# Moving four products of the output norm to VectorE in a decoder layer's last pass

## The chip, the cores and the metric

The kernel runs on one core of a Trainium2 chip. A core has TensorE (matmuls into PSUM), VectorE, ScalarE and GpSimd (elementwise work on SBUF; the first two also read PSUM), and queues that start transfers, of which SyncE's (SP) carries nearly all here. In the profile these are PE (with PEld for the loading of weights), DVE, ACT, POOL and SP. The metric is the device time of one execution in microseconds (us), the median of three runs.

## The reference

A decoder layer on `x` (256 tokens x 2048, float32): an attention part, then a feed-forward part, each as `x + rmsnorm(f(rmsnorm(x)))`. The change is in the end of the feed-forward part, here `y @ w_down` and the norm behind it:

```python
def rmsnorm(x, g):
    xf = x.astype(jnp.float32)
    y = xf * lax.rsqrt(jnp.mean(xf * xf, axis=-1, keepdims=True) + EPS)
    return (y * g.astype(jnp.float32)).astype(x.dtype)
...
    u = causal_dwconv(h @ w_up[l], conv_w[l], conv_b[l])
    gate, val = jnp.split(u, 2, axis=-1)
    y = (jax.nn.gelu(gate, approximate=True) * val) @ w_down[l]
    x = x + rmsnorm(y, post_ffn_g[l])
```

`w_down` is 5632 x 2048. The norm's gain `post_ffn_g` is a row of 2048 numbers, its mean one number per token.

## The kernel before

Float32 matmuls are made of three fp32r products: each operand is split into a high part (a cast on ScalarE) and a low part (source minus high part, on VectorE). For a weight tile these are `whi` and `wlo`; the helper `split` (L312, L313) makes both. A weight tile arrives in `raw` (5 buffers), `extra` (2) or the third part of `tb`, each 128 x 1024 and loaded by the SP queue.

The 5632 hidden columns are made in two halves. Behind each half come two passes over w_down, one for the output columns 0 to 1023 (`n == 0`) and one for 1024 to 2047 (`n == 2`); the sums of the first half wait in `y_sb` (two tiles `t` of 128 tokens, each of 2048 columns), to which those of the second half are added. Columns are counted in chunks of 512, so (t, n) is a token tile and chunk 0 to 3. `fast_pass` makes one pass: it goes through 11 units `u` of two weight tiles. Units 0, 2, 4 and 6 use a Strassen-like scheme with fewer products, whose combined sums (`m1`, `m5`, `m6`, `m7`, banks `bank_acc`) are spread over the outputs by `add_early` (L1121 to L1130); all others add products straight into four banks `late` (`bank_att`), one per (t, chunk).

In the very last pass the last three units (8, 9, 10) are held (`HOLD`): their split weights stay in SBUF, the last unit's in `rest`, and `block(0)` to `block(3)` multiply them at the end, one output block after the other: (0, 2), (0, 3), (1, 2), (1, 3). So the outputs come one by one, and the norm's work for one lies beside the matmuls of the next. Block (1, 3) is made in two halves of 256 columns.

What is done behind the blocks is written out from L1177 on. The order there is the program's on ScalarE, VectorE, GpSimd and SP (`manual_schedule`); before that line a scheduler places the instructions of these engines, except those under `keep_in_program_order`. TensorE's order is the program's throughout. The steps:

- `down(t, n, b, h)`: VectorE adds a bank to `y_sb` (L1087), ScalarE squares the result and sums the squares into `ysq[t]` (L1088).
- `gain(t, n, h, into)`: GpSimd multiplies a chunk of `y_sb` with the gain row `gbf` (L1154). All eight chunks are done so, (1, 3) in two parts, the second one into the tile `last`.
- `before_last(t, n)`: VectorE sums the first n partial sums of squares (L1160) and scales the sum (L1162); `rstd_y` adds the last one (L1167), and GpSimd raises the mean to the power -0.5 (L1169).
- `finish(t, cs, r, q, y)`: VectorE computes `y * r + x_back` (L1173, two tensor inputs in SBUF), and a queue stores it to the output. Tile 0 is finished in four steps of 512 columns, tile 1 in 512, 512, 512, 256, 256.
- `x_back` (the residual) and `gbf` are loaded by SP behind the last weights (L1182, L1184).

Of the kernel before, what the change touches and what calls it, by code (L numbers as in the profile page):

```python
# [8 lines left out]
F32 = mybir.dt.float32  # L9
# [3 lines left out]
ALU = mybir.AluOpType  # L13
# [4 lines left out]
P = 128  # L18
S = 256
D = 2048  # L20
# [11 lines left out]
def hybrid_layer(ctx: ExitStack, tc: tile.TileContext, x, pre_mix_g, w_in, b_forget, sinks,  # L32
# [3 lines left out]
    pe, act, dve, pool, sp = nc.tensor, nc.scalar, nc.vector, nc.gpsimd, nc.sync  # L36
# [7 lines left out]
    small = ctx.enter_context(tc.tile_pool(name="small", bufs=4))  # L44
# [4 lines left out]
    def bank(tag="acc"):  # L49
        return ps.tile([P, 512], F32, tag=tag, bufs=4, name="bank_" + tag)  # L50
# [13 lines left out]
    UNIT = 1024  # L64
# [66 lines left out]
    mhalf = const.tile([P, 1], F32, tag="mhalf", name="mhalf")  # L131
# [13 lines left out]
    for i in range(2):  # L145
        cs = slice(i * 256, (i + 1) * 256)
# [16 lines left out]
    junk = const.tile([P, 512], BF16, tag="junk", bufs=1, name="junk")  # L163
# [151 lines left out]
    with tc.tile_pool(name="mixp", bufs=1) as mp:  # L315
# [315 lines left out]
        for p0, npair, cols in ((0, 3, 384), (3, 3, 384), (6, 2, 272)):  # L631
# [13 lines left out]
            for t, b in enumerate(b2):  # L645
# [79 lines left out]
        gbc = hp.tile([P, D], F32, tag="gbc", name="gbc_mix")  # L725
# [121 lines left out]
    with tc.tile_pool(name="ffn", bufs=1) as fp:  # L847
# [24 lines left out]
        ROOM = 4128  # L872
# [95 lines left out]
                          stop=(last and i == 2))  # L968

        def fast_pass(G, sums, order, k00, c0, load, tb, early, late, add_early, hold=1,  # L970
                      keep=None):

            left, right = slice(0, 512), slice(512, UNIT)
            fast = [u for u in order if u in FAST]
# [19 lines left out]
            for u in order:  # L994
                k = 2 * u
                ra, rb = (load(w_rows(w_down, k00 + k + a, 1, c0, UNIT)) for a in range(2))
                if u in FAST:
# [26 lines left out]
                    if end and hold == 1:  # L1024
                        add_early()
                    continue
                b = [parts(r, UNIT, keep[a] if keep and u == order[-1] else None)
                     for a, r in enumerate((ra, rb))]
                if u in order[-hold:]:
                    held += [(k + a, b[a]) for a in range(2)]  # L1030
                    continue
# [17 lines left out]
        for half in range(2):  # L1049
# [4 lines left out]
            for g in range(FHALF // 2):  # L1054
# [10 lines left out]
                gates, ys = [], []  # L1065
# [18 lines left out]
            def down(t, n, b, h=None):  # L1084
                i, cs = (n, slice(0, 512)) if h is None else (n + h, slice(h * 256, h * 256 + 256))
                ys = y_sb[:, t, n * 512:(n + 1) * 512][:, cs]
                dve.tensor_tensor(ys, b[:, cs], ys, op=ALU.add)  # L1087
                act.activation(junk[:, cs], ys, AF.Square, accum_out=ysq[t][:, i:i + 1])  # L1088

            extra = fp.tile([P, 2, UNIT], F32, tag="gbc", name="extra")  # L1090
            tb = fp.tile([P, 3, UNIT], F32, tag="room", name="tb")
            spare = [extra[:, 0, :], extra[:, 1, :], tb[:, 2, :]]
            loads = [0]

# [8 lines left out]
            for n in (0, 2):  # L1103
# [28 lines left out]
                final = half and n  # L1132
                rest = None
                if final:
                    rest = main.tile([P, 2, 2, UNIT], F32R, tag="hT", name="rest")
                block = fast_pass(G, sums, order, half * FHALF, n * 512, load, tb, early, late,
                                  add_early, HOLD if final else 1,
                                  rest and [[rest[:, a, i, :] for i in range(2)]
                                            for a in range(2)])
# [11 lines left out]
        def gain(t, n, h=None, into=None):  # L1151
            cs = slice(0, 512) if h is None else slice(h * 256, h * 256 + 256)
            ys = y_sb[:, t, n * 512:(n + 1) * 512][:, cs]
            pool.tensor_tensor(ys if into is None else into, ys,  # L1154
                               gbf[:, n * 512:(n + 1) * 512][:, cs], op=ALU.mult)

        def before_last(t, n):

            st = small.tile([P, 1], F32, tag="st", name="st_y")
            dve.tensor_reduce(st, ysq[t][:, 0:n], axis=AX.X, op=ALU.add)  # L1160
            v = small.tile([P, 1], F32, tag="rv", name="rv")
            dve.tensor_scalar(v, st, 1.0 / D, EPS, op0=ALU.mult, op1=ALU.add)  # L1162
            return v

        def rstd_y(t, n, v):
            v2 = small.tile([P, 1], F32, tag="rv", name="rv")
            dve.scalar_tensor_tensor(v2, ysq[t][:, n:n + 1], 1.0 / D, v, op0=ALU.mult, op1=ALU.add)  # L1167
            r = small.tile([P, 1], F32, tag="ry", bufs=2, name="ry")
            pool.tensor_tensor(r, v2, mhalf, op=ALU.pow)  # L1169
            return r  # L1170

        def finish(t, cs, r, q, y=None):
# [7 lines left out]
        x_back = main.tile([P, 2, D], F32, tag="x", name="x_back")  # L1180
        for t in range(2):
            sp.dma_start(x_back[:, t, :], x_dram[t * P:(t + 1) * P, :])  # L1182
        gbf = fp.tile([P, D], F32, tag="gbc", name="gbc_ffn")
        sp.dma_start(gbf, post_ffn_g[0].partition_broadcast(P))  # L1184
        gain(0, 0)
        gain(0, 1)
        block(0)
        down(0, 2, late[0])
        gain(0, 2)
        gain(1, 0)  # L1190
        v = before_last(0, 3)
        block(1)
        down(0, 3, late[1])
        r = rstd_y(0, 3, v)
        gain(0, 3)
        gain(1, 1)
        for n in range(2):
            finish(0, slice(n * 512, (n + 1) * 512), r, sp)
        block(2)
# [2 lines left out]
        for n in range(2, 4):  # L1202
            finish(0, slice(n * 512, (n + 1) * 512), r, sp)
        last = fp.tile([P, 256], F32, tag="last", name="last")
        for h in range(2):
            if h:
                v = before_last(1, 4)
            b = bank()
            block(3, b, slice(512 + h * 256, 768 + h * 256))
            down(1, 3, b, h)  # L1210
            if h == 0:
                gain(1, 3, 0)
        r = rstd_y(1, 4, v)
# [33 lines left out]
```

## Time and profile before

| | |
|---|---|
| median of three runs | 1063.57 us (1063.05 to 1065.51) |
| span of the profiled execution, from first to last instruction (no other time of it is given) | 1062.6 us |
| TensorE busy in the span | 1049.6 us (99%) |
| VectorE | 839.7 us (79%) |
| ScalarE | 639.1 us (60%) |
| GpSimd | 229.3 us (22%) |
| mean granted TensorE clock | 0.996 |

A row of a timeline gives start, duration, engine, line, operation, output and inputs with their shapes, count, and in brackets the idle time of the engine ahead of it with what ended it. A row of several merged operations (x2, x4) gives their time together. [...] Shares of busy time are averages over the span, and here the last 12 us of it matter.

### The profile page before, as it was taken

How to read it: one execution, taken by the hardware profiler on the slowest of the kernel's cores; microseconds unless marked ns; L12 is line 12 of the kernel's file. 1: busy time of each engine (PE TensorE's matmuls, PEld its weight loads, DVE VectorE, ACT ScalarE, POOL GpSimd, SP SyncE). 2: the span in 40 equal slices, each digit the busy share in tenths (PEclk: the TensorE clock that was granted, in tenths of full speed). 3: DMA queues.
4: the chain of work that ended last, by engine and by line, in shares of the span. 5: the costliest groups of instructions: out<-in, count | busy, mean ns of one | idle time of the engine just before them, and what ended most of it. 6: DMA issues, size and time to landing. Idle time of an engine off the chain costs nothing.

```text
span 1062.6 us, 16272 instructions
## 1 busy us (share of the span) xinstructions
PE 1049.6 (99%) x5890; PEld 914.6 (86%) x5890; DVE 839.7 (79%) x1369; ACT 639.1 (60%) x1096; POOL 229.3 (22%) x256
## 2 busy tenths in 40 slices
PE   9999999999999999999999999999999999999996
PEld 7889988888889888888888888888888888888885
DVE  5988887887467887787767999668778687789987
ACT  6767667776556765566655556446556565556551
POOL 4253335441022121211212000002121121200004
PEclk9999999999999999999999999999999999999998
DMA  8745566555773876656665666666566665656563
GB/s 280 217 120 168 162 209 202 165 170 162 282 236 107 280 231 187 193 180 185 211 188 188 193 204 206 213 196 190 169 209 188 197 197 180 194 179 200 194 242 121
DMA packets 154285, 207.08 MB, mean 195 GB/s; under 512 B 6845, under 2 KB 131037, under 8 KB 153181
## 3 DMA queue, kind: packets, MB, share of 16 engines
q1 hardware_dynamic: 153200, 203.37, 60.7%
q10 hardware_dynamic: 1004, 2.68, 0.6%
q8 instruction: 46, 0.75, 0.3%
q14 instruction: 35, 0.28, 0.1%
HBM read 201.68 MB, written 4.21 MB: 194 GB/s over the span
## 4 chain that ended last, share of the span: by engine, by line
PE 84%; DVE 9%; issue 2%; DMA 2%; ACT 2%; POOL 1%; DVEq 0%; SPq 0%; POOLq 0%; ACTq 0%
PE bank_acc L284 15%; PE bank_att L284 14%; PE bank_acc L309 12%; PE bank_att L967 9%; PE bank_acc L290 8%; PE bank_att L290 7%; PE bank_acc L253 7%; DVE wlo L313 4%; PE bank_acc L258 4%; PE bank_acc L967 2%; PE bank_att L475 1%; PE bank_att L510 1%; DVE wlo L115 1%; PE bank_acc L932 1%; DMA raw<-in_w_down_dram 1%
## 5 line engine op out<-in xcount | busy, mean ns | idle before, releaser
L115 DVE TENSOR_TENSOR wlo<-raw,whi 128x1024 fp32r<-128x1024 f32 (+3 forms) x271 | 328.5, 1224 | 127.0 <-ACT whi L112 118.4
L112 ACT CAST whi<-raw 128x1024 fp32r<-128x1024 f32 (+3 forms) x270 | 273.2, 1029 | 131.8 <-issue 88.8
L899 POOL TENSOR_TENSOR room<-room,rowf 128x256 f32<-128x256 f32 x88 | 100.3, 1160 | 393.9 <-DVE room L898 392.0
L284 PE MATMUL bank_acc<-hT,whi 128*128 128x512 f32 x736 | 173.3, 390 | 0.0
L284 PEld LDWEIGHTS bank_acc<-hT,whi 128*128 128x128 f32 x736 | 136.4, 188 | 27.4
L967 PE MATMUL bank_att<-whi,G 128*128 128x512 f32 x488 | 156.0, 389 | 0.0
L284 PE MATMUL bank_att<-hT,whi 128*128 128x512 f32 x640 | 150.6, 390 | 0.0
L284 PEld LDWEIGHTS bank_att<-hT,whi 128*128 128x128 f32 x640 | 118.7, 188 | 23.9
L967 PEld LDWEIGHTS bank_att<-whi,G 128*128 128x128 f32 x488 | 91.6, 188 | 18.9
L967 PE MATMUL bank_att<-wlo,G 128*128 128x512 f32 x244 | 95.0, 389 | 0.2 <-DVE wlo L313 0.2
L290 PEld LDWEIGHTS bank_acc<-hT,wlo 128*128 128x128 f32 x736 | 89.3, 188 | 2.0
L290 PE MATMUL bank_acc<-hT,wlo 128*128 128x256 f32 x736 | 89.8, 279 | 0.0
L901 ACT ACTIVATE room<-room,cw 128x256 f32<-128x256 f32 x88 | 53.0, 602 | 60.6 <-POOL room L899 60.6
L253 PE MATMUL bank_acc<-hT,whi 128*128 128x512 f32 x352 | 88.0, 395 | 0.0
L309 PE MATMUL bank_acc<-whi,oT 128*128 128x512 f32 (+1 forms) x272 | 81.7, 379 | 0.0
L290 PEld LDWEIGHTS bank_att<-hT,wlo 128*128 128x128 f32 x640 | 77.6, 188 | 1.7
L290 PE MATMUL bank_att<-hT,wlo 128*128 128x256 f32 x640 | 77.9, 279 | 0.0
L903 DVE SCALAR_TENSOR_TENSOR room<-room,cw 128x256 f32<-128x256 f32 x88 | 62.4, 709 | 17.6 <-ACT room L901 17.3
L253 PEld LDWEIGHTS bank_acc<-hT,whi 128*128 128x128 f32 x352 | 63.3, 188 | 11.5
L313 DVE TENSOR_TENSOR wlo<-raw,whi 128x1024 fp32r<-128x1024 f32 (+1 forms) x56 | 61.3, 1119 | 12.1 <-ACT whi L312 12.1
L312 ACT CAST whi<-tb 128x1024 fp32r<-128x1024 f32 x42 | 44.0, 1050 | 43.0 <-PE bank_att L967 19.6
L312 ACT CAST whi<-raw 128x1024 fp32r<-128x1024 f32 (+1 forms) x56 | 52.3, 958 | 27.1 <-PE bank_att L967 20.6
(254 smaller groups left out, 1594.0 us busy)
## 6 DMA issues: line engine op xcount, KB each, us to landing
raw<-in_w_up_dram SPq DMA_DIRECT2D x176, 512.0 KB, 4.2
raw<-in_w_down_dram SPq DMA_DIRECT2D x58, 512.0 KB, 4.7
raw<-in_w_in_dram SPq DMA_DIRECT2D x51, 512.0 KB, 4.7
raw<-in_w_out_dram SPq DMA_DIRECT2D x32, 512.0 KB, 4.6
extra<-in_w_down_dram SPq DMA_DIRECT2D x20, 512.0 KB, 4.7
raw<-in_w_in_dram SPq DMA_DIRECT2D x16, 384.0 KB, 3.6
tb<-in_w_down_dram SPq DMA_DIRECT2D x10, 512.0 KB, 3.5
cb<-c_dram SPq DMA_DIRECT2D x8, 256.0 KB, 3.8
```

The source lines that it names most:

```text
L112: i1 = act.copy(hi[:, cs], raw[:, cs])
L115: i2 = dve.tensor_tensor(lo[:, cs], raw[:, cs], hi[:, cs].bitcast(F32), op=ALU.subtract)
L253: pe.matmul(b, parts[u][0][:, a, m * P:(m + 1) * P], hT[:, kt, :], start=(kt == 0), stop=(kt == KT - 1))
L284: pe.matmul(b, parts[u][0][:, a, m * P:(m + 1) * P], hT[:, kt, :], start=(kt == 0), stop=(kt == KT - 1))
L290: pe.matmul(b[:, 256:512], parts[u][1][:, a, m * P:(m + 1) * P], hT[:, kt, 0:256], start=False, stop=False)
L309: pe.matmul(b, a, r[:, cols], start=(first and i == 0), stop=(last and i == 2))
L312: act.copy(hi, src)
L313: dve.tensor_tensor(lo, src, hi.bitcast(F32), op=ALU.subtract)
L899: pool.tensor_tensor(u[:, 2:258], u[:, 2:258], rowf, op=ALU.mult)
L901: act.activation(y, u[:, 2:258], AF.Identity, bias=cw[:, 3, ch:ch + 1], scale=cw[:, 2, ch:ch + 1])
L903: dve.scalar_tensor_tensor(y, u[:, 1:257], cw[:, 1, ch:ch + 1], y, op0=ALU.mult, op1=ALU.add)
L967: pe.matmul(b[:, to] if to else b, a, r[:, cols], start=(first and i == 0), stop=(last and i == 2))
```

## The change

Four things are changed.

1. The products with the gain for chunks 0 and 1 of both token tiles are made by VectorE inside the last pass, one each in units 7, 8, 9 and 10 (`early_gain`, called as `beside` in `fast_pass`). Their values are complete since the pass before. GpSimd keeps (0, 2), (0, 3), (1, 2) and the first half of (1, 3).
2. The gain row is loaded in two halves: columns 0 to 1023 into `gb_lo`, free room behind `tb`, on SP before the last pass; columns 1024 to 2047 where the whole row was loaded before.
3. The mean is no longer taken in two steps for token tile 0: `before_last(0, 4)` sums all four parts after the last square.
4. For the last 256 columns of tile 1 VectorE squares and sums in one operation (`tensor_tensor_reduce`, with the sum of the earlier columns `v` as its start) instead of ScalarE, and VectorE instead of GpSimd makes the product `last`, behind it.

```diff
@@ fast_pass
+                      keep=None, beside=None):
...
                 b = [parts(r, UNIT, keep[a] if keep and u == order[-1] else None)
                      for a, r in enumerate((ra, rb))]
+                if beside:
+                    beside(u)
                 if u in order[-hold:]:
@@ behind each half
             extra = fp.tile([P, 2, UNIT], F32, tag="gbc", name="extra")
-            tb = fp.tile([P, 3, UNIT], F32, tag="room", name="tb")
+            rest_room = fp.tile([P, ROOM], F32, tag="room", name="tb")
+            tb = rest_room[:, 0:3 * UNIT].rearrange("p (a c) -> p a c", a=3)
+            gb_lo = rest_room[:, 3 * UNIT:4 * UNIT]
...
                 final = half and n
                 rest = None
                 if final:
+                    sp.dma_start(gb_lo, post_ffn_g[0, 0:UNIT].partition_broadcast(P))
+
+                def early_gain(u):
+                    if u in (7, 8, 9, 10):
+                        t, c = divmod(u - 7, 2)
+                        ys = y_sb[:, t, c * 512:(c + 1) * 512]
+                        tc.keep_in_program_order(
+                            dve.tensor_tensor(ys, ys, gb_lo[:, c * 512:(c + 1) * 512], op=ALU.mult))
+
+                if final:
                     rest = main.tile([P, 2, 2, UNIT], F32R, tag="hT", name="rest")
...
+                                  final and early_gain)
@@ gain
-                               gbf[:, n * 512:(n + 1) * 512][:, cs], op=ALU.mult)
+                               gbf[:, (n - 2) * 512:(n - 1) * 512][:, cs], op=ALU.mult)
@@ the root
-        def rstd_y(t, n, v):
-            v2 = small.tile([P, 1], F32, tag="rv", name="rv")
-            dve.scalar_tensor_tensor(v2, ysq[t][:, n:n + 1], 1.0 / D, v, op0=ALU.mult, op1=ALU.add)
+        def root(ms):
             r = small.tile([P, 1], F32, tag="ry", bufs=2, name="ry")
-            pool.tensor_tensor(r, v2, mhalf, op=ALU.pow)
+            pool.tensor_tensor(r, ms, mhalf, op=ALU.pow)
             return r
@@ behind the pass
-        gbf = fp.tile([P, D], F32, tag="gbc", name="gbc_ffn")
-        sp.dma_start(gbf, post_ffn_g[0].partition_broadcast(P))
-        gain(0, 0)
-        gain(0, 1)
+        gbf = fp.tile([P, UNIT], F32, tag="gbc", name="gbc_ffn")
+        sp.dma_start(gbf, post_ffn_g[0, UNIT:D].partition_broadcast(P))
         block(0)
         down(0, 2, late[0])
         gain(0, 2)
-        gain(1, 0)
-        v = before_last(0, 3)
         block(1)
         down(0, 3, late[1])
-        r = rstd_y(0, 3, v)
+        r = root(before_last(0, 4))
         gain(0, 3)
-        gain(1, 1)
...
-        for h in range(2):
-            if h:
-                v = before_last(1, 4)
-            b = bank()
-            block(3, b, slice(512 + h * 256, 768 + h * 256))
-            down(1, 3, b, h)
-            if h == 0:
-                gain(1, 3, 0)
-        r = rstd_y(1, 4, v)
-        gain(1, 3, 1, last)
+        b = bank()
+        block(3, b, slice(512, 768))
+        down(1, 3, b, 0)
+        gain(1, 3, 0)
+        v = before_last(1, 4)
+        b = bank()
+        block(3, b, slice(768, UNIT))
+        ys = y_sb[:, 1, D - 256:D]
+        dve.tensor_tensor(ys, b[:, 256:512], ys, op=ALU.add)
+        ms = small.tile([P, 1], F32, tag="ms", bufs=1, name="ms")
+        dve.tensor_tensor_reduce(junk[:, 0:256], ys, ys, 1.0 / D, v, ALU.mult, ALU.add, ms)
+        r = root(ms)
+        dve.tensor_tensor(last, ys, gbf[:, UNIT - 256:UNIT], op=ALU.mult)
```

The lines behind the edits have new numbers: `add_early`'s adds L1123 to L1130 are L1127 to L1134 in the changed kernel, L1087 (the add in `down`) is L1089, the add of the last block's early part L1141 is L1156, L1173 (`finish`) is L1186, and the new products are L1146.

TensorE's, ScalarE's and the queue's orders stay as they were, but for the load of `gb_lo`, one square fewer on ScalarE, and new line numbers. On VectorE the order changes in two places. The first is the end of the last pass. Before (each row: line, operation, output and inputs with the buffer's number, shape):

```order
L313 TENSOR_TENSOR wlo_10470<-extra_9717,whi_10469 128x1024
L313 TENSOR_TENSOR wlo_10500<-extra_9717,whi_10499 128x1024
L313 TENSOR_TENSOR rest_10178<-raw_10521,rest_10178 128x1024
L313 TENSOR_TENSOR wlo_10504<-tb_9718,whi_10503 128x1024
L313 TENSOR_TENSOR wlo_10512<-raw_10507,whi_10511 128x1024
L1123 TENSOR_TENSOR y_sb_3944<-s_10527,y_sb_3944 128x512
L313 TENSOR_TENSOR wlo_10516<-raw_10509,whi_10515 128x1024
L1124 TENSOR_TENSOR s_10527<-bank_acc_10173,s_10527 128x512
```

The first row is the low part of unit 7's second weight tile, the next `wlo` rows and the `rest` row belong to the held units. The same place after:

```order
L313 TENSOR_TENSOR wlo_10471<-extra_9717,whi_10470 128x1024
L1146 TENSOR_TENSOR y_sb_3944<-y_sb_3944,tb_9718 128x512
L313 TENSOR_TENSOR wlo_10502<-extra_9717,whi_10501 128x1024
L313 TENSOR_TENSOR rest_10179<-raw_10525,rest_10179 128x1024
L313 TENSOR_TENSOR wlo_10506<-tb_9718,whi_10505 128x1024
L1146 TENSOR_TENSOR y_sb_3944<-y_sb_3944,tb_9718 128x512
L313 TENSOR_TENSOR wlo_10515<-raw_10510,whi_10514 128x1024
L313 TENSOR_TENSOR wlo_10519<-raw_10512,whi_10518 128x1024
L1146 TENSOR_TENSOR y_sb_3944<-y_sb_3944,tb_9718 128x512 x2
L1127 TENSOR_TENSOR y_sb_3944<-s_10532,y_sb_3944 128x512
```

Two products stand ahead of the last `wlo`, two behind it, and the first add of `add_early` has moved behind all of them. A few rows on, the add of the first held sums (`bank_att_10174`) stands ahead of the last three steps of `add_early`, where before it stood behind them. The second place is the end of the program, VectorE before:

```order
L1160 TENSOR_REDUCE st_y_10651<-ysq1_3946 128x1
L1162 TENSOR_SCALAR rv_10653<-st_y_10651 128x1
L1087 TENSOR_TENSOR y_sb_3944<-bank_acc_10655,y_sb_3944 128x256
L1167 SCALAR_TENSOR_TENSOR rv_10676<-ysq1_3946,rv_10653 128x1
L1173 SCALAR_TENSOR_TENSOR y_sb_3944<-y_sb_3944,ry_10678,x_back_10540 128x512 x3
```

and after, where ISA stands for the one operation that squares and sums, and for the read of its sum:

```order
L1175 TENSOR_REDUCE st_y_10650<-ysq1_3946 128x1
L1177 TENSOR_SCALAR rv_10652<-st_y_10650 128x1
L1221 TENSOR_TENSOR y_sb_3944<-bank_acc_10654,y_sb_3944 128x256
L1223 ISA junk_98,ms_10674<-y_sb_3944,rv_10652 128x256
L1223 ISA ms_10674 128x1
L1225 TENSOR_TENSOR last_10627<-y_sb_3944,gbc_ffn_10548 128x256
L1186 SCALAR_TENSOR_TENSOR y_sb_3944<-y_sb_3944,ry_10676,x_back_10545 128x512 x3
```

The wait for ScalarE's square (ahead of L1167) is gone, two VectorE instructions take its place, and the product `last` has moved here from the end of GpSimd's row.

More of the change, by code (lines that the diff above doesn't have):

```diff
@@ L970, in fast_pass @@
         def fast_pass(G, sums, order, k00, c0, load, tb, early, late, add_early, hold=1,
-                      keep=None):
+                      keep=None, beside=None):
             left, right = slice(0, 512), slice(512, UNIT)
@@ L1138, in hybrid_layer @@
                                   rest and [[rest[:, a, i, :] for i in range(2)]
-                                            for a in range(2)])
+                                            for a in range(2)],
+                                  final and early_gain)
                 if final:
```

## The prediction

> **What bounds the kernel now.** I read the page first, then the busy time by stage, then the end of the chain of waits, and last the timelines of the engines from 1020 us on, since the order of instructions shows that nothing before the last pass over w_down is moved except one load.
>
> ```profile
> span 1062.6 us, 16272 instructions
> PE 1049.6 (99%) x5890; PEld 914.6 (86%) x5890; DVE 839.7 (79%) x1369; ACT 639.1 (60%) x1096; POOL 229.3 (22%) x256
> ...
> 1000.00:1029.40 29.40, 29.40 (x131) 24.36 (x130) 24.92 (x29) 16.00 (x19) 0.00 (x0) 1.00 0.62 215
> 1039.40:1052.10 12.70, 12.67 (x73) 11.02 (x71) 10.85 (x15) 2.17 (x6) 9.05 (x7) 1.00 0.10 41
> 1052.10:1062.60 10.50, 0.00 (x0) 0.00 (x0) 4.92 (x11) 1.02 (x4) 3.48 (x4) 0.64 0.42 152
> ...
> 1052.14 2.24 POOL y_sb L1154 x2
> ```
>
> The three middle rows are stretches of time: length, then busy time (and count) of PE, PEld, DVE, ACT, POOL. TensorE is full to 1052.1 us and has nothing to do in the last 10.5 us. So a gain can come from only two places: TensorE's end, which the change does not shorten (its instructions are the same, in the same order), and the 10.5 us behind it. The last row is one of the chain of waits: of those 10.5 us, 2.24 go through two products on GpSimd (L1154). The span is the profiled execution's only time given; the runs' median of 1063.57 us is 0.97 us above it (lowest 0.45, highest 2.9 above), so I work on the span and add 0.97. A difference of about 0.2%, 2.1 us, is what a measurement of this kernel can tell from no change.
>
> The end of VectorE's work, operation by operation (start, duration, engine, line):
>
> ```profile
> 1045.71 0.81 DVE L1167 SCALAR_TENSOR_TENSOR rv<-ysq,rv 128x1 f32<-128x1 f32 x1 [0.85 <-ACT junk L1088]
> 1047.18 1.77 DVE L1173 SCALAR_TENSOR_TENSOR y_sb<-y_sb,ry,x_back 128x512 f32<-128x512 f32 x1 [0.66 <-POOL ry L1169]
> 1050.57 0.68 DVE L1087 TENSOR_TENSOR y_sb<-bank_att,y_sb 128x512 f32<-128x512 f32 x1
> 1051.17 1.40 DVE L1173 SCALAR_TENSOR_TENSOR y_sb<-y_sb,ry,x_back 128x512 f32<-128x512 f32 x2
> 1052.49 0.41 DVE L1087 TENSOR_TENSOR y_sb<-bank_acc,y_sb 128x256 f32<-128x256 f32 x1
> 1053.54 0.16 DVE L1160 TENSOR_REDUCE st_y<-ysq 128x1 f32<-128x4 f32 x1 [0.64 <-ACT junk L1088]
> 1053.80 0.41 DVE L1087 TENSOR_TENSOR y_sb<-bank_acc,y_sb 128x256 f32<-128x256 f32 x1
> 1054.79 0.16 DVE L1167 SCALAR_TENSOR_TENSOR rv<-ysq,rv 128x1 f32<-128x1 f32 x1 [0.57 <-ACT junk L1088]
> 1055.61 1.20 DVE L1173 SCALAR_TENSOR_TENSOR y_sb<-y_sb,ry,x_back 128x512 f32<-128x512 f32 x1 [0.66 <-POOL ry L1169]
> 1056.74 0.74 DVE L1173 SCALAR_TENSOR_TENSOR y_sb<-y_sb,ry,x_back 128x512 f32<-128x512 f32 x1
> 1058.46 0.47 DVE L1173 SCALAR_TENSOR_TENSOR y_sb<-last,ry,x_back 128x256 f32<-128x256 f32 x1
> ```
>
> The last sums of TensorE are added at 1053.80, 1.7 us after TensorE ended: VectorE is late, not TensorE. The same 512-column finishing step takes 1.77, 0.70 (half of 1.40) and 1.20 us. What stretches it is on GpSimd:
>
> ```profile
> 1043.96 2.54 POOL L1154 TENSOR_TENSOR y_sb<-y_sb,gbc_ffn 128x512 f32<-128x512 f32 x2 [0.28 <-ACT junk L1088]
> 1047.11 1.29 POOL L1154 TENSOR_TENSOR y_sb<-y_sb,gbc_ffn 128x512 f32<-128x512 f32 x1
> 1048.36 1.74 POOL L1154 TENSOR_TENSOR y_sb<-y_sb,gbc_ffn 128x512 f32<-128x512 f32 x1
> 1055.03 0.55 POOL L1169 TENSOR_TENSOR ry<-rv,mhalf 128x1 f32<-128x1 f32 x1 [0.65 <-DVE rv L1167]
> 1055.54 0.72 POOL L1154 TENSOR_TENSOR last<-y_sb,gbc_ffn 128x256 f32<-128x256 f32 x1
> ```
>
> A VectorE operation with both inputs in SBUF that starts inside a GpSimd product ends 0.55 us after the product: product to 1048.40, finishing step to 1048.95; product to 1056.26, step to 1056.81. The other way round, the product begun at 1048.36 beside that step takes 1.74 instead of 1.29. The add from PSUM at 1053.80 keeps its 0.41 beside a product. So the two engines exclude each other, for such operations only.
>
> The last pass on VectorE, ScalarE and TensorE:
>
> ```profile
> 1027.56 1.22 DVE L313 TENSOR_TENSOR rest<-raw,rest 128x1024 fp32r<-128x1024 f32 x1 [3.06 <-ACT rest L312]
> 1028.70 1.22 DVE L313 TENSOR_TENSOR wlo<-raw,whi 128x1024 fp32r<-128x1024 f32 x1
> 1035.52 0.68 DVE L1123 TENSOR_TENSOR y_sb<-s,y_sb 128x512 f32<-128x512 f32 x1
> 1036.12 1.22 DVE L313 TENSOR_TENSOR wlo<-raw,whi 128x1024 fp32r<-128x1024 f32 x1
> 1037.26 0.68 DVE L1124 TENSOR_TENSOR s<-bank_acc,s 128x512 f32<-128x512 f32 x1
> 1041.47 1.05 DVE L1130 TENSOR_TENSOR y_sb<-s,y_sb 128x512 f32<-128x512 f32 x1
> 1042.44 0.68 DVE L1087 TENSOR_TENSOR y_sb<-bank_att,y_sb 128x512 f32<-128x512 f32 x1
> 1044.17 0.68 DVE L1087 TENSOR_TENSOR y_sb<-bank_att,y_sb 128x512 f32<-128x512 f32 x1
> ...
> 1026.48 1.05 ACT L312 CAST rest<-raw 128x1024 fp32r<-128x1024 f32 x1 [3.24 <-DMA raw<-in_w_down_dram]
> ...
> 1029.98 0.50 PE L967 MATMUL bank_att<-wlo,G 128*128 128x512 f32 x1 [0.17 <-DVE wlo L313]
> 1030.32 0.39 PE L967 MATMUL bank_att<-whi,G 128*128 128x512 f32 x1
> 1037.60 0.39 PE L967 MATMUL bank_att<-wlo,G 128*128 128x512 f32 x1
> 1037.83 0.40 PE L967 MATMUL bank_att<-whi,G 128*128 128x512 f32 x1
> 1051.19 0.88 PE L967 MATMUL bank_acc<-rest,G 128*128 128x256 f32 x6
> ```
>
> A late load ends ScalarE's wait at 1026.48, VectorE's at 1027.56, and TensorE waits at 1029.98 for VectorE. From there VectorE has no gap and TensorE no slack worth the name.
>
> **The change, part by part.**
>
> *Four products on VectorE in the last pass.* One such operation moves the row on by 0.60 us (1035.52 to 1036.12), so four cost 2.4 us. None falls into the 3.06 us gap: in the new order the first stands behind the low part of `extra`, two are ahead of the last low part (`wlo`), two behind it. Two times 0.60 ahead, and L1123 (0.60) no longer there, puts the last `wlo` at 1036.72 instead of 1036.12; it ends at 1037.94, and TensorE wants it at 1037.60. TensorE will wait: late by 0.34 plus 0.06 for the signal (1028.70+1.22 = 1029.92 against 1029.98). At 1029.98 a wait of this kind shows as 0.17 of idle time, and the next matmul follows after 0.34 instead of 0.23 (1037.60 to 1037.83): 0.3 for the smaller lateness there. I take 0.5 us here, so TensorE ends near 1052.6. This costs the end nothing while VectorE reaches the last add later than that.
>
> *VectorE's row behind it.* The next operation comes 1.14 us after the last `wlo` starts (1036.12 to 1037.26), so at 1037.86; two more products bring L1127 to 1039.06. Four steps of the old row took (1041.47 minus 1037.26)/6 = 0.70 each; L1128 to L1131 and then the add of the first held sums, which now stands ahead of the last three steps, make five: about 1042.5, as before (1042.44). L1132 to L1134 follow at 1043.1, 1043.8, 1044.5. GpSimd's first product now is that of (0, 2), started by the same add as before, so 1043.96 to 1045.25; L1134 has two SBUF inputs and ends 0.55 later, at 1045.80. L1156 and the second add (before: 1044.17) then start at 1045.83 and 1046.44: 2.27 us late.
>
> *First root.* Behind the add (0.68): square on ScalarE with its signals 0.8 to 0.86 (the add of 1044.17 ends at 1044.85, L1167 starts at 1045.71), now reduce and scale behind it, 0.34 (1053.54 to 1053.80, plus 0.08 until the result is out; before it was L1167 alone, which took 0.81 instead of 0.16, being held by GpSimd's product to 1046.50), root and signals 0.66 (1054.95 to 1055.61). The first finishing step starts at about 1048.95, before 1047.18. GpSimd's product (0, 3) starts 0.07 before it, as at 1047.11, so at 1048.88, so one step is blocked (ends 1050.72), not two; the second takes 0.74. The add of the third sums comes at 1051.27, before 1050.57: of 2.4 us, one blocked step fewer (1.03) and L1167's wait (0.65) have given back all but 0.70. The same 0.70 holds for what follows: the last add at 1054.50.
>
> *The last 256 columns.* Before, from the end of the add (1054.21) by ScalarE's square and L1167 (to 1054.95): 0.74 us. Now one operation and the read of its sum. Its nearest rows, from attention, have one input in PSUM:
>
> ```profile
> L481 DVE CUSTOM_DVE_ANT_0 p<-bank_att,p x32: 259/340/426, 165.5 to 252.7; 128x256 f32<-128x256 f32 x16, 128x128 f32<-128x128 f32 x16
> L481 DVE DVE_READ_ACCUMULATOR2_ANT nm<- x64: 72/83/86, 47.2 to 253.0; 128x1 f32 x64
> ```
>
> The longest, the 128x256 form, is 0.42; with 0.08 and 0.03 it saves 0.2. It may be blocked by the product of (1, 3), which by the same shift runs to 1055.08: 0.05 more, to 1055.49. Root 0.08 + 0.55 + 0.03: the first finishing step at 1056.15. `last` now is made by VectorE under the root. Either it costs nothing, or the root, which reads SBUF, waits for the rest of it: bounds 0 and 0.25 (0.41 less its earlier start). The row at 1048.36, a GpSimd operation lengthened by 0.45, is the nearest, so 0.2. The first finishing step, no longer blocked, hands over after 0.66: the second starts at 1056.81 to 1057.0, before 1056.74. From there all is as before. Sum: **+0.07 without, +0.27 with the wait of the root; I take +0.2**, a span of 1062.8.
>
> [...]
>
> *Loads.* The gain row's first half (512 KB) is loaded by the SP queue ahead of two others:
>
> ```profile
> 944.53 0.33 SPq L69 DMA_DIRECT2D raw<-in_w_down_dram  x1
> 949.41 2.67 SPq L1100 DMA_DIRECT2D extra<-in_w_down_dram  x2
> ```
>
> The queue stands still for 4.9 us there; at 215 GB/s 512 KB take 2.4. Cost nothing, and if that cover were gone at most 2.4 us on one load that TensorE does not wait for. The later load of gains is halved; it was no wait on the path.
>
> **Rivals.**
>
> *Faster: no pair blocks.* If L1134 (0.55), the finishing step (1.03) and the root (0.2) met no product in progress, the last add would come 1.6 earlier, at 1052.9, just behind TensorE's end. Span 1061.0, time about 1062.0. For it: starts within 0.07 us of each other decide who holds whom. Against it: in the old run the product won each time. It lies inside 0.2%; another 0.6 us, from TensorE not waiting and the runs falling low, would pass it.
>
> *Slower: a late load.* The load that ScalarE waited for until 1026.48 lands one transfer of 512 KB later, because the added load shifts the queue: 2.4 us, passed on by VectorE and TensorE alike, as neither has slack there: time 1066.2. It decides from 2 us. Against it: the added load is 75 us earlier, and the queue idles after it.
>
> *TensorE becomes the bound.* It would need a wait over 1.9 us (1054.50 against 1052.6); 0.5 is expected.
>
> **How the numbers follow.** Forecast as summed, 0.78; no pair blocks, 0.11; late load, 0.06; TensorE bound or drift of the runs, 0.05. The predicted time is 1062.8 + 0.97 = 1063.8. The low end is the faster rival's 1062.0; the high end takes the forecast with the runs' upper spread (1065.5) and most of the way to the late load: 1065.7. Faster by over 0.2%: half of the faster rival, with the 0.6 us that it lacks, 0.06. Slower: the late load and a little drift, 0.07. Within: the rest, 0.87.
>
> **What would show it.** Right: four L1146 rows of 0.69 between 1030 and 1039; a TensorE wait for `wlo` near 1037.7; the second add of held sums at 1046.4; the first two finishing steps at 1.8 and 0.7 us; the step behind the last root at 0.74, not 1.20; the last finishing step within 0.4 us of 1058.46. Wrong: a root that starts well before or after 1055.6, a wait of TensorE above 1.9 us, a product begun after the finishing step, or ScalarE's load wait ending later than 1026.5.

## The result: 0.5% slower, and TensorE is 7 us longer at work

The changed kernel takes 1070.22 us (median of 5 runs, 1068.96 to 1070.42); the kernel before 1064.15 us (5 runs, 1063.05 to 1066.43). The ratio is 1.0051, with a 95% interval of 1.0041 to 1.0062; the ratios given here are estimates with their own intervals, not quotients of the medians. The forecast was no change, 1063.8 us.

The head of the page of the changed kernel, with span and busy times as they were shown of before:

```profile
span 1068.7 us, 16272 instructions
PE 1056.8 (99%) x5890; PEld 914.5 (86%) x5890; DVE 841.6 (79%) x1374; ACT 639.2 (60%) x1094; POOL 220.7 (21%) x251
```

The same 5890 matmuls keep TensorE busy for 7.2 us longer (1056.8 against 1049.6). So the first thing to read is TensorE by groups of equal instructions; the last two columns ahead of the bar and behind it are the busy time of a group in us, and the mean of one in ns. Before:

```profile
L284 PE MATMUL bank_acc<-hT,whi 128*128 128x512 f32 x736 | 173.3, 390 | 0.0
L967 PE MATMUL bank_att<-whi,G 128*128 128x512 f32 x488 | 156.0, 389 | 0.0
L967 PE MATMUL bank_att<-wlo,G 128*128 128x512 f32 x244 | 95.0, 389 | 0.2 <-DVE wlo L313 0.2
L309 PE MATMUL bank_acc<-whi,oT 128*128 128x512 f32 x240 | 75.5, 391 | 0.0
L309 PE MATMUL bank_acc<-wlo,oT 128*128 128x512 f32 x120 | 46.7, 389 | 0.0
L309 PE MATMUL bank_acc<-whi,hT 128*128 128x384 f32 x128 | 33.9, 338 | 0.0
```

After:

```profile
L284 PE MATMUL bank_acc<-hT,whi 128*128 128x512 f32 x736 | 173.3, 390 | 0.0
L967 PE MATMUL bank_att<-whi,G 128*128 128x512 f32 x488 | 159.2, 395 | 0.0
L967 PE MATMUL bank_att<-wlo,G 128*128 128x512 f32 x244 | 96.4, 395 | 0.0
L309 PE MATMUL bank_acc<-whi,oT 128*128 128x512 f32 x240 | 76.8, 396 | 0.0
L309 PE MATMUL bank_acc<-wlo,oT 128*128 128x512 f32 x120 | 47.4, 395 | 0.0
L309 PE MATMUL bank_acc<-whi,hT 128*128 128x384 f32 x128 | 33.9, 338 | 0.0
```

A row names the moving tile first (512 columns of it in most of these) and then the stationary tile, the weights (128 x 128). The projections (L284, moving tile `hT`) and the parts of L309 with the stationary tile `hT` are the same to 0.1 us. Every group of 512 columns whose stationary tile is `oT` (the output projection) or `G` (the passes over w_down) takes 5 to 7 ns more for each instruction; these four rows add 6.6 us. None of it lies where the change was made: the output projection is over by 340 us, and half of the passes over w_down belong to the first half of the hidden columns.

It is no wait and no clock. In the timeline of TensorE, six steps of 512 columns at about the same time, in the second half's passes, before and then after (start, duration, in which neighbours overlap; a step is the time from one start to the next):

```profile
959.83 0.62 PE L967 MATMUL bank_acc<-whi,sums 128*128 128x512 f32 x2
...
961.19 0.62 PE L967 MATMUL bank_att<-whi,G 128*128 128x512 f32 x2
```

```profile
959.79 0.63 PE L967 MATMUL bank_att<-whi,G 128*128 128x512 f32 x2
960.25 0.40 PE L967 MATMUL bank_att<-wlo,G 128*128 128x512 f32 x1
960.49 0.63 PE L967 MATMUL bank_att<-whi,G 128*128 128x512 f32 x2
960.96 0.40 PE L967 MATMUL bank_att<-wlo,G 128*128 128x512 f32 x1
961.19 0.63 PE L967 MATMUL bank_att<-whi,G 128*128 128x512 f32 x2
```

Six steps take 961.19 - 959.83 = 1.36 us before, 0.2267 each, and 961.19 - 959.79 = 1.40 after, 0.2333 each. No row has an idle time in brackets. The stretches around them (columns as in the prediction; before, then after) have a granted clock of 1.00, and fewer matmuls in the same full 100 us:

```profile
600.00:700.00 100.00, 100.00 (x450) 83.11 (x449) 82.82 (x93) 54.12 (x57) 0.20 (x4) 1.00 0.63 207
```

```profile
600.00:700.00 100.00, 100.00 (x432) 80.73 (x431) 81.63 (x93) 51.85 (x55) 0.20 (x4) 1.00 0.62 205
```

Stage by stage, from the start of a stage's first matmul to that of its last in the two traces: the output projection 95.79 us before and 97.80 after, the passes over w_down of the first half 114.01 and 116.99, those of the second half 114.85 and 117.17. TensorE's last work ends at 1052.07 before and 1059.32 after (+7.25); what is left behind it is 10.52 and 9.36 (-1.16). Together that is the 6.1 us of the span.

What differs in those places is where the tiles lie. The changed kernel asks for one tile more in the pool `small`: `ms`, one number per partition, under a tag of its own. It takes 32 bytes, and every pool that is opened behind `small` moves by them. Byte addresses within a partition in the two built programs:

```
                                       before    after
first tile of G   (weights, L967)      174080   174112
first tile of oT  (weights, L309)      153088   153120
raw, whi, wlo, hT, rest, sums, y_sb    as before
whi and wlo kept for oT8 to oT15       +32, as oT
```

The distance from the stationary to the moving tile (`whi`, `wlo`, `rest`) was a multiple of 256 bytes in both products, and now has 32 bytes more. Only a few `whi` and `wlo` that the output projection keeps for its last products lie in a pool behind `small` and move with `oT`. Their 24 steps of 512 columns take 226.9 ns in the changed kernel, against 233.2 for the other 325 of that stage, so its trace holds both cases. In the projections of L284 both tiles are where they were.

### The profile page after: what moved, and what is told of

It is laid out like the page before. It is cut to its first block, busy times and chain, and to the rows that moved or that the text cites. A ratio compares the mean times of both kernels' runs of the same rounds, so it can differ in the third digit from the quotient of the medians.

```text
span 1068.7 us, 16272 instructions
## 1 busy us (share of the span) xinstructions
PE 1056.8 (99%) x5890; PEld 914.5 (86%) x5890; DVE 841.6 (79%) x1374; ACT 639.2 (60%) x1094; POOL 220.7 (21%) x251
## 4 chain that ended last, share of the span: by engine, by line
PE 91%; DVE 4%; DMA 1%; ACT 1%; issue 1%; POOL 1%; SPq 0%; DVEq 0%; POOLq 0%; ACTq 0%
PE bank_acc L284 16%; PE bank_att L967 15%; PE bank_att L284 14%; PE bank_acc L309 12%; PE bank_acc L290 8%; PE bank_att L290 7%; PE bank_acc L253 7%; PE bank_acc L967 4%; PE bank_acc L258 4%; PE bank_att L475 1%; DVE wlo L313 1%; PE bank_att L510 1%; DVE wlo L115 1%; PE bank_acc L932 1%; DMA raw<-in_w_down_dram 1%
## 5 line engine op out<-in xcount | busy, mean ns | idle before, releaser
L112 ACT CAST whi<-raw 128x1024 fp32r<-128x1024 f32 (+3 forms) x270 | 273.3, 1030 | 132.6 <-issue 88.8
L284 PE MATMUL bank_acc<-hT,whi 128*128 128x512 f32 x736 | 173.3, 390 | 0.0
L284 PEld LDWEIGHTS bank_acc<-hT,whi 128*128 128x128 f32 x736 | 136.4, 188 | 27.4
L967 PE MATMUL bank_att<-whi,G 128*128 128x512 f32 x488 | 159.2, 395 | 0.0
L284 PE MATMUL bank_att<-hT,whi 128*128 128x512 f32 x640 | 150.6, 390 | 0.0
L284 PEld LDWEIGHTS bank_att<-hT,whi 128*128 128x128 f32 x640 | 118.7, 188 | 23.9
L309 PE MATMUL bank_acc<-whi,oT 128*128 128x512 f32 (+1 forms) x272 | 83.0, 384 | 0.0
```

The lines of the kernel that those rows point to most:

```text
L112: i1 = act.copy(hi[:, cs], raw[:, cs])
L284: pe.matmul(b, parts[u][0][:, a, m * P:(m + 1) * P], hT[:, kt, :], start=(kt == 0), stop=(kt == KT - 1))
L309: pe.matmul(b, a, r[:, cols], start=(first and i == 0), stop=(last and i == 2))
L967: pe.matmul(b[:, to] if to else b, a, r[:, cols], start=(first and i == 0), stop=(last and i == 2))
```

## Experiments: is it the 32 bytes, or the edits?

Two theories stood against each other. The first: TensorE's step depends on where the stationary and the moving tile lie to each other, and the edits themselves cost what the prediction says. The second: it is the edits (more work on VectorE, another load, other orders), and the addresses have nothing to do with it.

**The edits without the 32 bytes.** `ms` takes a buffer of the tag that is there already, and nothing else moves.

```diff
-        ms = small.tile([P, 1], F32, tag="ms", bufs=1, name="ms")
+        ms = small.tile([P, 1], F32, tag="rv", name="ms")
```

> The changed kernel whole, but its new one-number tile (ms) takes a buffer of the tag rv, as the tile before it did, so that nothing behind the pool small lies 32 bytes further on. Theory A (the 32 bytes slow TensorE where its weights are G or oT): the matmul step in the passes over w_down is 0.227 us again, TensorE ends near 1052.1 to 1052.6, and the time is that of before less about 1 us: 1062.5 to 1064, ratio 0.998 to 1.000. Theory B (the moved work itself slows TensorE's stages, as contention or through the loads): nothing of it is undone, so the step stays 0.232 to 0.235 and the time 1069 to 1070.5.

Measured: 1063.95 us (11 runs, 1063.33 to 1065.79), before 1063.92; ratio 1.0001, 0.9992 to 1.0009. The three stages take 95.79, 114.01 and 115.26 us. So the whole slowdown hangs on the place of one small tile.

**The 32 bytes without the edits.** The kernel before, with one tile that nothing uses:

```diff
     small.tile([P, 112], F32, tag="room", bufs=1, name="room_s")
+    small.tile([P, 1], F32, tag="pad", bufs=1, name="pad")
```

> The kernel before with one unused tile of one number more in the pool small, which puts oT, G and all behind them 32 bytes further on; no instruction is changed. Theory A: all of TensorE's loss without the change: a step of 0.232 to 0.235 in the output projection and the passes over w_down, TensorE ends 7 us later, time 1070 to 1072, ratio 1.006 to 1.008. Theory B: no difference, ratio 0.999 to 1.001.

Measured: 1070.77 us (4 runs, 1070.41 to 1071.64); ratio 1.0063, 1.0047 to 1.0078. The stages take 97.80, 116.99 and 117.17 us, those of the changed kernel to 0.01. Its steps at the same time of the trace, four rows that are 0.23 to 0.24 apart for each matmul:

```profile
959.65 0.40 PE L968 MATMUL bank_att<-wlo,G 128*128 128x512 f32 x1
959.89 0.63 PE L968 MATMUL bank_att<-whi,G 128*128 128x512 f32 x2
960.36 0.40 PE L968 MATMUL bank_att<-wlo,G 128*128 128x512 f32 x1
...
961.05 0.40 PE L968 MATMUL bank_att<-wlo,G 128*128 128x512 f32 x1
```

From 959.65 to 961.05 are six steps: 0.2333 each. The second theory falls with these two runs: the edits without the shift cost nothing, and the shift without the edits costs all of it.

**Which shifts?** With 64 bytes in the place of 32:

```diff
+    small.tile([P, 16], F32, tag="pad", bufs=1, name="pad")
```

> The kernel before with an unused tile of 64 bytes more in the pool small. Theory A1 (what counts is the address modulo 64 bytes): as before, step 0.227, ratio 0.999 to 1.001. Theory A2 (what counts is the distance from the weights to the moving tiles, or a round address): step 0.232 or more, ratio above 1.004. Theory B: no difference.

Measured: 1071.63 us (4 runs); ratio 1.0068, 1.0055 to 1.0082; 0.2332 for a step of 512 columns with `G`. A grid of 64 bytes is refuted.

**A sweep in one kernel.** The tiles of `G` are made 2080 bytes apart instead of 2048, so each lies 32 bytes further off than the one ahead of it:

```diff
-            G = [fp.tile([P, 512], F32R, tag="G", bufs=FHALF, name=f"G{j}") for j in range(FHALF)]
+            G = [fp.tile([P, 520], F32R, tag="G", bufs=FHALF, name=f"G{j}")[:, 0:512]
+                 for j in range(FHALF)]
```

> The kernel before with the 22 tiles G 2080 bytes apart instead of 2048, so that their addresses modulo 64 are 0 and 32 in turn, and modulo 2048 all different. Theory A1: within one pass, half of the tiles take 0.227 us a matmul and the other half 0.232 to 0.235, whatever their place modulo 2048. Theory A2: some other pattern along the tiles. Theory B: 0.227 for all.

Measured: 1067.5 us (one run); the passes take 116.49 us in the first half and 116.70 in the second, the output projection, whose tiles did not move, 95.79. The steps, worked out from the matmuls' starts, by the address of the weights modulo 512 (that of the moving tile is a multiple of 256 throughout; steps next to a change of tile are left out):

```
weights mod 512     0     32     64     96    128    160    192    224
steps              44     31     19     73     73     49     33     40
mean, ns        227.1  232.4  233.9  234.2  232.9  234.2  229.7  233.2

weights mod 512   256    288    320    352    384    416    448    480
steps              40     16      4     40     40     16      4     40
mean, ns        226.7  232.7  236.0  234.2  233.3  234.2  231.8  233.2
```

The step is short at a distance of 0 and of 256 bytes, and long or nearly so at the other fourteen. It is one run, and some columns have few steps.

**A shift of 256 bytes**, then, should cost nothing:

```diff
-    small.tile([P, 112], F32, tag="room", bufs=1, name="room_s")
+    small.tile([P, 176], F32, tag="room", bufs=1, name="room_s")
```

> The kernel before with 256 bytes more in an unused tile of the pool small, so that oT, G and all behind them lie 256 bytes further on. Theory A with 256 bytes as the unit: as before, step 0.227, ratio 0.999 to 1.001. Rival (the distance to the moving tiles counts, or a larger unit such as 512 or 2048): a step of 0.231 or more, ratio above 1.004.

Measured: 1064.72 us (10 runs, 1063.35 to 1065.28), before 1064.05; ratio 1.0001, 0.9992 to 1.001. The sweep's reading holds.

**The place itself, or the distance?** 32 bytes put ahead of all pools, so that weights and moving tiles go together:

```diff
-    const.tile([P, 120], F32, tag="room", name="room_c")
+    const.tile([P, 128], F32, tag="room", name="room_c")
```

> The kernel before with 32 bytes more in an unused tile of the first pool, const, so that everything behind it in SBUF, moving tiles and weights alike, lies 32 bytes further on and their distances stay. Theory A-absolute (a weight tile has to start at a multiple of 256 bytes to be loaded at full speed): TensorE's step for 512 columns goes from 0.227 to 0.231-0.235 in all stages, the up-projection's too, whose weights were aligned so far; some 3500 such steps by 0.0067 make 1080 to 1090 us. Theory A-relative (what counts is where the weights lie against the moving tiles): nothing changes, 1063 to 1066 us.

Measured: 1064.85 us (one run), and a mean of 0.2267 for the 794 steps of 512 columns with `G`. Its rows at the same time:

```profile
959.71 0.62 PE L967 MATMUL bank_acc<-whi,sums 128*128 128x512 f32 x2
...
961.07 0.62 PE L967 MATMUL bank_att<-whi,G 128*128 128x512 f32 x2
```

Six steps, 1.36 us: as before the change, although every tile lies 32 bytes off its old place. It is the distance.

**The distance from the other side.** Only the low moving tile `wlo` moves, by 32 bytes in the room that it has:

```diff
-        c = LOW if still else 0
+        c = LOW if still else 8
```

> The kernel before with the low parts of the moving weights (wlo, where they are the moving operand: output projection, value projection and the passes over w_down) 32 bytes further on inside their buffers; the stationary tiles G and oT stay. Theory A-absolute: only the stationary operand counts, step 0.227, time as before, 1063 to 1066 us. Theory A-relative: the steps of the products with wlo, one in three, become slower, by a third of the loss: about 1066 to 1067 us.

Measured: 1069.78 us (one run), more than the 1066 to 1067 expected. The steps with `G` and `wlo` take 0.2329 (260 of them), and those with `whi`, whose tiles are at a multiple of 256 as ever, 0.2311 (519) instead of the 0.2267 before: the neighbours of a product with the wrong distance are drawn out too. In the changed kernel the same holds for the products with `sums`, whose own distance is unchanged: 0.2267 before and 0.2303 after. How one step hands this to the next, the starts don't tell.

**Can the rule be used for a gain?** The products of the projections with 256 columns take `wlo` as the stationary tile, at an offset of 56 numbers, 224 bytes. Put at 0, they have the distance that is short above:

```diff
-    LOW = 56
+    LOW = 0
```

> The kernel before with LOW = 0: the low parts of the projections' weights start at a multiple of 256 bytes instead of 224 bytes behind one, as the moving tile hT does. If the rule of equal addresses modulo 256 bytes holds for the products with 256 columns too, the low products there (step 0.113 to 0.120 us) become shorter, and the time falls by up to 1 us per 150 such steps, 5 to 10 us in all. If it holds only for 512 columns, where loading the next weights lies beside a longer stream, the time stays at 1063 to 1066 us or rises.

Measured: 1067.63 us, before 1064.62 (one run each): 3 us slower, where by the rule it should have been faster. The groups, before and then with the offset 0:

```profile
L290 PE MATMUL bank_acc<-hT,wlo 128*128 128x256 f32 x736 | 89.8, 279 | 0.0
L290 PE MATMUL bank_att<-hT,wlo 128*128 128x256 f32 x640 | 77.9, 279 | 0.0
```

```profile
L290 PE MATMUL bank_acc<-hT,wlo 128*128 128x256 f32 x736 | 92.1, 283 | 0.0
L290 PE MATMUL bank_att<-hT,wlo 128*128 128x256 f32 x640 | 79.9, 283 | 0.0
```

Each takes 4 ns more; nearly all their steps are 0.120 us now, where before they were between 0.113 and 0.120. So the rule of 256 bytes stands for products of 512 columns behind weights of 128 x 128, where it was measured, and not for those of 256 columns. The length of the moving row alone can turn it. The last block over w_down, (1, 3), multiplies the same `G`, `whi`, `wlo` and `rest` in pieces of 256 columns, and its 35 steps take 119.8 ns in the kernel before (distance 0), 118.6 in the changed one (32 bytes) and 113.5 with 64 bytes, the run in which the steps of 512 columns rise to 233.2. It is no plain reversal: the six distances of this block in the sweep, five or six steps each, gave 117.2 to 122.5.

**The two halves of the edits apart**, both without the extra 32 bytes. The products and loads alone, with the old end (square on ScalarE, `last` on GpSimd):

```diff
-        b = bank()
-        block(3, b, slice(512, 768))
...
-        dve.tensor_tensor(last, ys, gbf[:, UNIT - 256:UNIT], op=ALU.mult)
+        for h in range(2):
...
+        r = rstd_y(1, 4, v)
+        gain(1, 3, 1, last)
```

> The change's four early products (with the halved gain row and the first root after the last square) without its end: ScalarE squares the last 256 columns and GpSimd makes the product last, as before; no new tile. By my sum: TensorE waits once for wlo (0.4 to 0.5 us) and VectorE's last add stands 0.5 to 0.7 us later than in the kernel before, the rest being the same; counted from TensorE's end the span's rest is 10.5 to 10.8 us (before 10.52). Rival (the products relieve VectorE of GpSimd's exclusion and so pay): 9.5 to 10.0 us.

Measured: 1065.93 us (one run), 10.72 us behind TensorE's end. The span of this run is longer by a load: TensorE's waits for `wlo` sum to 1.4 us in it, so only the part behind TensorE's end is compared.

The end alone, with the products and loads as before:

```diff
+        ms = small.tile([P, 1], F32, tag="rv", name="ms")
+        dve.tensor_tensor_reduce(junk[:, 0:256], ys, ys, 1.0 / D, v, ALU.mult, ALU.add, ms)
...
+        dve.tensor_tensor(last, ys, gbf[:, D - 256:D], op=ALU.mult)
```

> The kernel before with only the end of the change: the last 256 columns squared and summed by one VectorE operation (ms in the tag rv) and the product last on VectorE. By my sum: from the last add to the second finishing step 2.4 to 2.6 us instead of 2.94, so a rest of 10.0 to 10.2 us behind TensorE's end (before 10.52). Rival (the root waits for the product last, and nothing is saved): 10.4 to 10.6 us.

Measured: 1064.31 us (one run; before 1064.62), 9.90 us behind TensorE's end, against 10.52 before, a little under the 10.0 to 10.2 expected: the end is worth 0.6 us of it. Some 0.1 of that is TensorE ending closer to VectorE's last add; from that add to the end of the span it is 8.27 us instead of 8.79. With both halves 10.15 are left, so the products as placed give back 0.2 of that. Differences of this size come from one profile each and are a reading of rows, not a measured ratio.

**The same products in slack.** The prediction says that VectorE has no gap from the late load on, and that none of the four products falls ahead of it. So they are put into units 1, 3, 5 and 7 of the pass, three of them ahead of it, again without the extra 32 bytes:

```diff
-                    if u in (7, 8, 9, 10):
-                        t, c = divmod(u - 7, 2)
+                    if u in (1, 3, 5, 7):
+                        t, c = divmod((1, 3, 5, 7).index(u), 2)
```

> The changed kernel with ms in the tag rv (so TensorE at full speed) and the four early products in units 1, 3, 5 and 7 of the last pass instead of 7 to 10; nothing else differs. If VectorE's backlog behind the late load is what the products cost (my sum): TensorE no longer waits for the last wlo, VectorE reaches the held sums 1.8 us earlier (three products fewer behind the late load), and the end comes about 1 to 1.5 us earlier than with the products late: 1062.4 to 1063.2, ratio to before 0.9980 to 0.9995. Rival (the end hangs on TensorE and on the exclusion of GpSimd and VectorE, not on the products): ratio 1.000.

Measured: 1061.53 us (11 runs, 1060.5 to 1063.2), before 1064.05; ratio 0.9979, 0.997 to 0.9988. It is the fastest of all, 0.2% below the kernel before, and lower than expected: some 2.3 us below the run with the products late (0.9979 against 1.0001), not 1 to 1.5. Of its operations on VectorE, the fourth product with the gain and the add of the last sums:

```profile
1028.74 0.68 DVE L1146 TENSOR_TENSOR y_sb<-y_sb,tb 128x512 f32<-128x512 f32 x1
...
1051.66 0.41 DVE L1221 TENSOR_TENSOR y_sb<-bank_acc,y_sb 128x256 f32<-128x256 f32 x1
```

TensorE ends at 1051.18, so VectorE is 0.5 us behind it at the last add, where before it was 1.7 behind. 8.65 us are left behind TensorE's end, where with the products late it was 10.15, and TensorE never waits for `wlo`. Two things have moved, though. Three of the four products now stand ahead of VectorE's last gap (they start at 999.31, 1009.27 and 1019.25, the gap ends at 1024.19). And the scheduler has placed the splits of the last units in another order, so that ScalarE does not wait for the late load here (its wait to 1023.11, of 4.12 us, is for VectorE's `tb`). VectorE comes to the first add of `add_early` at 1036.15 instead of 1037.91, and this 1.76 us is what three products of 0.60 take; but no run separates the products from the new order.

## Why the prediction was wrong

The step that failed is this one: "a gain can come from only two places: TensorE's end, which the change does not shorten (its instructions are the same, in the same order)". TensorE was taken as untouched in the sum and in every rival, on the strength of its order. The order shows instructions and names, not addresses. The term that was set to 0 measured +7.25 us. The times of the sum behind the late load were off by no more than 0.2, as shown below. The rival "TensorE becomes the bound" looked for a wait above 1.9 us; TensorE did become the bound, by its own step and without a wait, in stages that the prediction had ruled out as unmoved. Its 0.05 was a chance for another thing.

The step went from 0.2267 us before to 0.2333 after with the distance of the two tiles; why the distance counts, no run here shows.

The rest of the sum can be checked in the run with `ms` in the old tag, where TensorE has its full pace. In its profile the late load that ScalarE waits for ends at 1025.34 instead of 1026.48, and what follows hangs on it:

```profile
1025.34 1.05 ACT L312 CAST rest<-raw 128x1024 fp32r<-128x1024 f32 x1 [3.06 <-DMA raw<-in_w_down_dram]
...
1036.85 0.50 PE L967 MATMUL bank_att<-wlo,G 128*128 128x512 f32 x1 [0.18 <-DVE wlo L313]
...
1034.44 2.35 DVE L313 TENSOR_TENSOR wlo<-raw,whi 128x1024 fp32r<-128x1024 f32 x2
1036.71 1.29 DVE L1146 TENSOR_TENSOR y_sb<-y_sb,tb 128x512 f32<-128x512 f32 x2
1043.34 1.31 DVE L1134 TENSOR_TENSOR y_sb<-s,y_sb 128x512 f32<-128x512 f32 x1
1045.30 0.68 DVE L1089 TENSOR_TENSOR y_sb<-bank_att,y_sb 128x512 f32<-128x512 f32 x1
1047.83 2.43 DVE L1186 SCALAR_TENSOR_TENSOR y_sb<-y_sb,ry,x_back 128x512 f32<-128x512 f32 x2 [0.66 <-POOL ry L1182]
1053.42 0.41 DVE L1221 TENSOR_TENSOR y_sb<-bank_acc,y_sb 128x256 f32<-128x256 f32 x1
1053.87 0.48 DVE L1223 CUSTOM_DVE_ANT_0 junk<-y_sb,rv 128x256 bf16<-128x256 f32 x1
1055.14 2.47 DVE L1186 SCALAR_TENSOR_TENSOR y_sb<-y_sb,ry,x_back 128x512 f32<-128x512 f32 x4 [0.44 <-POOL ry L1182]
```

With these 1.14 us added, point by point:

- Last `wlo`: the second of the pair ends at 1036.79 and so starts at 1035.57, with the shift 1036.71; forecast 1036.72. TensorE waits for it, as forecast, and ends at 1051.47, shifted 1052.61; forecast 1052.6.
- L1134 is held by GpSimd's product (1.31 us instead of 0.69, its end 0.55 behind that of the product); the second add of held sums at 1046.44; forecast 1046.44.
- One of the first two finishing steps is held, not two: 2.43 us for the pair, where the next two take 1.40; forecast 1.8 and 0.7.
- The last add at 1054.56; forecast 1054.50. Square and sum in one operation 0.48; forecast 0.42, from a row with one input in PSUM.
- The first step behind the last root at 1056.28; forecast 1056.15. The four steps from there take 2.47 us; by the old run's rows they took 2.92 (first of them held).
- Span 1061.62, shifted 1062.76; forecast 1062.8. Median 1063.95; forecast 1063.8. That the median agrees so well is partly luck: the 0.97 us that the prediction adds to the span compares a median with the span of another execution, while each run here takes 1.7 us more than its own span (1063.33 with 1061.6, 1063.95 with 1062.2). The middle span of the eleven runs is 0.6 below the forecast 1062.8, and the two misses cancel.

The wait of the root that was taken at 0.2 us of a possible 0 to 0.25 is there at half the price. The last root of the changed kernel, on GpSimd, against 0.55 us for its first:

```profile
1054.29 0.55 POOL L1182 TENSOR_TENSOR ry<-rv,mhalf 128x1 f32<-128x1 f32 x1 [3.15 <-DVE rv L1177]
...
1061.48 0.66 POOL L1182 TENSOR_TENSOR ry<-ms,mhalf 128x1 f32<-128x1 f32 x1 [0.44 <-DVE ms L1223]
```

The other rivals. "No pair blocks" did not come: the pairs that the sum holds for blocked are blocked in the rows above. "A late load" did not come either: ScalarE's wait for it ends at 1025.34 and 1027.42 with the added load (here and in the run with the products alone) and at 1026.48 and 1027.10 without it (the kernel before and the run with the end alone). The four profiles spread by 2.1 us, with no side to it.

In the changed kernel itself the prediction's times between 1030 and 1059 can't be found at all, as TensorE is 5 to 7 us late there. Its slowness even hides part of the change: the trace has no wait of TensorE for `wlo`, VectorE is 1.1 us behind TensorE at the last add instead of 1.7 (1060.46 against 1059.32), and 9.36 us are left at the end, less than in the run with TensorE at full pace (10.15). That may be why the bytes alone measured somewhat more than the whole change (1.0063 and 1.0051); the intervals overlap, so the runs don't show it.

## What to carry to other kernels

A new tile is part of a change even if it is one number wide: compare the addresses of all tiles before and after, not only the order of the instructions, and give small tiles a tag or a place that moves nothing. Where TensorE is the bound with products of 512 columns like these, keep stationary and moving tiles a multiple of 256 bytes apart (0.2267 us a step here, against 0.230 to 0.234; products of 256 columns did not follow this), and look at the mean duration of one matmul by group: a few ns more in groups that the diff does not touch (5 to 7 here), at full clock and without a wait, point to this. Work that is moved to a busy engine belongs ahead of the point from which that engine has no gap; a few units earlier, the same edits went from no gain (1.0001) to 0.2% (0.9979), with the order of the splits changed as well.

## What was not expected of the hardware

- In the products with `G` a matmul of 512 columns stepped on in 0.2267 us (the kernel before, and the run with everything moved by 32 bytes) where its weights and its moving tile lay a multiple of 256 bytes apart, and in 0.230 to 0.234 (the sweep) at the other distances tried (32, 64, 96, 128, 160, 192, 224 bytes modulo 256). Some 1130 products lie at a wrong distance in the changed kernel, 257 us at 0.2267 or about a quarter of the kernel; 3% of that makes 0.7%.
- It was the distance that counted, not the place (a mean of 0.2267 over 794 steps with all moved), and a product with a wrong distance also drew out its neighbours (0.2311, in the run with `wlo` moved).
- For 256 columns it was not so: in the projections an offset of 224 bytes gave 0.113 to 0.120 us, an offset of 0 gave 0.120; in the last block over w_down, with the same tiles as the products of 512 columns, a distance of 0 gave 0.1198 and one of 64 bytes 0.1135. Why the length of the moving row changed it is open.
- A one-column operation on GpSimd, the last root, took 0.66 us beside a VectorE product of 256 columns with both inputs in SBUF (the changed kernel, the run with `ms` in the old tag), and 0.55 without one (the first root in both, the last root before).
